# The first steps of a triangular inverse on compact 32x32 blocks instead of 128x128 matrices

## The chip, the cores and the metric

The kernel runs on one core of one Trainium2 chip. The metric is the device time of one execution in microseconds (us). A TensorE product is written as weights (lhsT) and a moving operand (rhs) and lands in PSUM; VectorE (DVE), ScalarE (ACT) and GpSimd (POOL) work on SBUF and PSUM, and the transfers from HBM are issued by SyncE (SP).

## The reference

One block and two further layers over 256 tokens of width 1024, in fp32. The block modulates a normed x, projects it, mixes it (a gMLP half and an RWKV7 half), and runs a mixture of 32 experts; the two layers are attention and a feed-forward part each. The change is inside the RWKV7 half, a recurrence over 256 steps for 8 heads of 64:

```python
def step(state, inp):
    r_t, w_t, k_t, v_t, a_t, b_t = inp
    sa = jnp.einsum('bhvk,bhk->bhv', state, a_t)
    state = (state * w_t[:, :, None, :] + sa[..., None] * b_t[:, :, None, :]
             + v_t[..., None] * k_t[:, :, None, :])
    return state, jnp.einsum('bhvk,bhk->bhv', state, r_t)
```

## The kernel before

The recurrence is computed in two chunks of 128 steps. Within a chunk the sa of each step depends on those of the steps before it through a strictly triangular 128x128 matrix N, so the kernel needs the inverse of I − N for each of 8 heads and 2 chunks, 16 matrices ("slots"). NT holds N transposed, for all slots side by side: a tile of 128 partitions and 16 times 128 columns. XT holds the inverse transposed as it grows, Y its transpose block by block.

The inverse is built by doubling. First come the 2x2 diagonal blocks, from N masked by offT plus the identity, made by POOL (L749, L750) one head at a time. Four levels follow, l from 1 to 4, which double the finished blocks to 4, 8, 16 and 32: a product N·Y (L782), a mask off[l] on it that keeps the new off-diagonal blocks and gives W (L798), a product X·W added to X (L800), and a transposition of the 32x32 blocks that gives Y for the next level (L791). Before, each of these works on whole 128x128 matrices in four groups of four slots (one PSUM bank, 512 columns), although of X and Y only the four 32x32 blocks on the diagonal hold anything yet. Behind the levels two further doublings go from 32 to 64 (the function blocks, L810, on 32x32 pieces of the array, with WC as the copy in between) and from 64 to 128 (L829 to L837). The finished XT is first used at L887.

The order of the instructions on each engine is made ahead of time by a scheduler that goes by priority and dependence; each engine then works through its list in order. Between the stages of the kernel stand fills: fill(n) draws n steps of a generator that computes modulation vectors, products of a vector with a weight matrix (L190), whose weights are loaded 1 MB at a time (wrows) into six slots. A step is 8 matmuls on four column strips of the array in turn. fill(FILL_A[2]), two steps, stands at the head of each level, fill(FILL_A[5]) behind them. A step's sum leaves PSUM through ACT (L230) or DVE (L232, ga), and after every fourth step DVE transposes the vector (L196, gt) and adds a bias (L197, modc). The same six slots, in program order, take the loads of the output projection and of the experts later.

The product L744 (AR, BP) makes N; L758 (AR, KP) makes the other matrix of the chunk, which DVE masks (L761, ma) and L765 and L766 multiply with V. These stand between the making of N and the first level.

## Time and profile before

| | |
|---|---|
| median of 3 runs | 1437.48 us (1435.19 to 1439.3) |
| profiled execution, its own time | 1440.6 us |
| its span in the trace | 1438.8 us |
| mean granted TensorE clock | 0.98 |
| TensorE busy | 94% of the span |
| VectorE busy | 53% |
| ScalarE busy | 40% |
| GpSimd busy | 5% |

The span runs from the first to the last instruction of the profiled execution; its own time has what lies around that. The shares are over the whole kernel, which has stages with very different limits, so what a change in one stage is worth must be read from the windows and timelines of that stage. An fp32 matmul leaves two records for its products (and two for its weight loads): counts of matmuls in the profile are twice those of the program. The granted clock is a share of 2.4 GHz, so that 0.50 is 1.2 GHz.

### The profile page before, as it was taken

What the parts mean: (1) busy time and instruction counts of PE and PEld (TensorE: products, weight loads), DVE (VectorE), ACT (ScalarE), POOL (GpSimd) and SP (SyncE); (2) the same over time, 40 slices, a digit from 0 to 9 for tenths busy, and PEclk for the clock granted to TensorE, in tenths of its full rate; (3) what the DMA queues carried; (4) which work ended last, traced back from release to release, by engine and by line L of the source; (5) the groups of instructions that cost most, each with busy time, mean ns of one, the idle gap of its engine ahead of it and who ended that gap; (6) DMA issues with size and microseconds to landing.
All of it is one profiled execution on the core that took longest, in us unless ns stands there. A gap on an engine that the chain in (4) does not pass through costs nothing.

```text
span 1438.8 us, 22940 instructions
## 1 busy us (share of the span) xinstructions
PE 1358.0 (94%) x9327; PEld 996.0 (69%) x9327; DVE 765.7 (53%) x1510; ACT 572.8 (40%) x1020; POOL 73.1 (5%) x77
## 2 busy tenths in 40 slices
PE   7989999999999988999889989999998999999997
PEld 5778887544443434444348867899996897799997
DVE  5639667511211111111165875888876575766565
ACT  3444013311110111111166765555456685655544
POOL 1002000000000000000020231000021001100000
PEclk9979999999999999999989999999999999999999
DMA  9817379699999999999956554978775434555540
GB/s 354 302 59 264 137 288 386 252 358 426 426 428 425 427 427 424 427 427 425 426 223 247 207 204 154 350 273 315 276 248 185 160 118 152 192 192 196 178 145 30
DMA packets 138690, 400.44 MB, mean 278 GB/s; under 512 B 6561, under 2 KB 84657, under 8 KB 114002
## 3 DMA queue, kind: packets, MB, share of 16 engines
q1 hardware_dynamic: 138578, 398.91, 72.1%
q8 instruction: 75, 1.23, 0.3%
q14 instruction: 37, 0.30, 0.1%
HBM read 397.82 MB, written 1.05 MB: 277 GB/s over the span
## 4 chain that ended last, share of the span: by engine, by line
PE 45%; DMA 9%; DVE 3%; ACT 2%; issue 1%; POOL 0%; POOLq 0%; DVEq 0%; SPq 0%; ACTq 0%
PE pmm L416 8%; PE pmm L417 8%; PE pmm L418 8%; PE pacc L416 5%; PE pacc L417 5%; PE pacc L418 5%; DMA wruns<-in_moe_w_down_dram 4%; DMA wruns<-in_moe_w_gate_dram 3%; DMA wruns<-in_moe_w_up_dram 3%; PE pmm L190 1%; PE pmm L1346 1%; PE pmm L1302 1%; DVE x_sb L1495 1%; PE pmm L366 1%; PE pmm L1705 1%
## 5 line engine op out<-in xcount | busy, mean ns | idle before, releaser
L416 PE MATMUL pmm<-hh,whi 128*128 128x256 f32 (+1 forms) x1040 | 296.0, 285 | 2.0 <-ACT whi L167 2.0
L418 PE MATMUL pmm<-hh,wlo 128*128 128x256 f32 (+1 forms) x1040 | 297.0, 286 | 0.0
L417 PE MATMUL pmm<-hl,whi 128*128 128x256 f32 (+1 forms) x1040 | 295.7, 284 | 0.0
L1302 PE MATMUL pmm<-wruns,xg 128*64 128x512 f32 x1024 | 232.6, 595 | 10.6 <-DMA wruns<-in_moe_w_gate_dram 9.0
L168 DVE TENSOR_TENSOR wlo<-wcols,whi 128x1024 fp32r<-128x1024 f32 (+1 forms) x130 | 168.4, 1300 | 97.4 <-ACT whi L167 96.9
L416 PEld LDWEIGHTS pmm<-hh,whi 128*128 128x128 f32 (+1 forms) x1040 | 197.5, 190 | 8.5 <-issue 3.6
L417 PEld LDWEIGHTS pmm<-hl,whi 128*128 128x128 f32 (+1 forms) x1040 | 196.6, 189 | 1.4
L418 PEld LDWEIGHTS pmm<-hh,wlo 128*128 128x128 f32 (+1 forms) x1040 | 197.1, 189 | 0.3
L167 ACT ACTIVATE whi<-wcols 128x1024 fp32r<-128x1024 f32 (+1 forms) x130 | 136.0, 1052 | 115.8 <-PE pmm L417 91.3
L1302 PEld LDWEIGHTS pmm<-wruns,xg 128*64 128x64 f32 x1024 | 75.3, 137 | 150.1 <-issue 127.6
L168 DVE TENSOR_TENSOR wlo<-wrows,whi 128x1024 fp32r<-128x1024 f32 x87 | 108.1, 1248 | 53.8 <-ACT whi L167 53.4
L167 ACT ACTIVATE whi<-wrows 128x1024 fp32r<-128x1024 f32 x87 | 91.6, 1061 | 89.6 <-PE pmm L417 46.4
L1346 PE MATMUL pmm<-wruns,em 128*64 128x512 f32 x512 | 118.8, 595 | 5.5 <-DMA wruns<-in_moe_w_down_dram 4.1
L1346 PEld LDWEIGHTS pmm<-wruns,em 128*64 128x64 f32 x512 | 38.3, 137 | 78.1 <-issue 61.3
L1355 ACT ACTIVATE o<-ay 128x512 fp32r<-128x512 f32 x32 | 20.2, 630 | 172.7 <-DVE ay L1354 172.7
L1354 DVE SCALAR_TENSOR_TENSOR ay<-pmm,wsl,ga 128x512 f32<-128x512 f32 x32 | 24.0, 751 | 101.7 <-PE pmm L1346 99.7
L1388 DVE TENSOR_TENSOR ay<-ay,pmm 128x512 f32<-128x512 f32 x16 | 11.0, 688 | 119.2 <-PE pmm L1302 105.8
L1333 DVE COPY wsl<-pmm 64x1 f32<-64x1 f32 x32 | 5.0, 156 | 126.6 <-PE pmm L1330 126.4
L417 PE MATMUL pacc<-wlo,ah 128*128 128x512 f32 x176 | 69.2, 393 | 0.0
L416 PE MATMUL pacc<-whi,ah 128*128 128x512 f32 x176 | 68.9, 391 | 0.0
L418 PE MATMUL pacc<-whi,al 128*128 128x512 f32 x176 | 68.6, 393 | 0.0
L1308 ACT ACTIVATE ay<-pmm 128x512 f32<-128x512 f32 x16 | 9.6, 598 | 109.3 <-PE pmm L1302 109.3
(530 smaller groups left out, 2190.2 us busy)
## 6 DMA issues: line engine op xcount, KB each, us to landing
wruns<-in_moe_w_gate_dram SPq DMA_DIRECT2D x64, 1024.0 KB, 19.5
wruns<-in_moe_w_up_dram SPq DMA_DIRECT2D x64, 1024.0 KB, 19.5
wruns<-in_moe_w_down_dram SPq DMA_DIRECT2D x64, 1024.0 KB, 19.6
wrows<-in_w_mod_dram SPq DMA_DIRECT2D x48, 1024.0 KB, 6.9
wcols<-in_w_ffn_gate_dram SPq DMA_DIRECT2D x22, 1024.0 KB, 5.1
wcols<-in_w_ffn_up_dram SPq DMA_DIRECT2D x22, 1024.0 KB, 7.2
wrows<-in_w_ffn_down_dram SPq DMA_DIRECT2D x22, 1024.0 KB, 4.9
wrows<-in_ada_w_dram SPq DMA_DIRECT2D x16, 1024.0 KB, 7.5
```

The source lines that it names most:

```text
L167: ACT.activation(hi, src, AF.Copy)
L168: (POOL if ahead else DVE).tensor_tensor(lo, src, hi.bitcast(F32), op=OP.subtract)
L190: PE.matmul(p[32 * g:32 * g + 32, 0:n].rearrange("p (a j) -> p a j", j=32), lhsT, groups(rhs)[:, g], start=first, stop=last, skip_group_ch ...
L366: PE.matmul(p, src[:, i, 128 * kt:128 * kt + 128], dg[i], start=True, stop=True)
L416: PE.matmul(p, a[0], b[0], start=first, stop=False, skip_group_check=True)
L417: PE.matmul(p, a[0], b[1], start=False, stop=False, skip_group_check=True)
L418: PE.matmul(p, a[1], b[0], start=False, stop=last, skip_group_check=True)
L1302: PE.matmul(p[64 * a:64 * a + 64, :], xg[:, kt, 128 * (j % 2) + 64 * a:128 * (j % 2) + 64 * a + 64], wt[a][:, k, :], start=kt == 0, stop=k ...
L1346: PE.matmul(pd[n][64 * a:64 * a + 64, :], hT[:, f, 64 * a:64 * a + 64], wt[a][:, b, 512 * n:512 * n + 512], start=f == 0, stop=f == 3, ski ...
L1354: DVE.scalar_tensor_tensor(yf, pd[n], wsl, ga2[:, ns], op0=OP.mult, op1=OP.mult)
L1355: ACT.activation(oh[:, ns], yf, AF.Copy)
L1495: DVE.scalar_tensor_tensor(xs, t[:, i, half_[n]], r[i], xs, op0=OP.mult, op1=OP.add)
```

## The change

The 2x2 blocks and the four levels are done on the diagonal 32x32 blocks alone. X3, Y3 and W3 hold them compactly, one tile of 128 partitions by 8 slots of 32 columns for each of two groups g of eight slots; block r of a matrix lies on partitions 32r to 32r+31. begin(g) copies the diagonal blocks out of NT with ACT, masks them, adds the identity and transposes, all on DVE; POOL's part goes. A level has two groups instead of four. products(g) runs 32 matmuls of 32x32x32 for a group, with the block r innermost: four in a row go to the four diagonal 32x32 places of the array and write four partition strips of one PSUM bank. DVE's operations on a level are 128x256 instead of 128x512, two of each kind instead of four. The masks off, offT are 128x32 (five instead of six), with an added identity idc. Behind the levels the products of the step to 64 read Y3 and X3 and are written slot by slot, so that two or three places of the array take turns; eight ACT copies bring the blocks of X3 into the full XT, which POOL has cleared, and four those of Y3 into a tile YW that holds Y and W of the last doubling.

On TensorE, before, a level and the fills around it stand like this (pacc<-wrows is a fill; each x16 of pmm is four groups of four slots); the first level has 6 of its 16 first products ahead of the fill:

```order
L190 MATMUL pacc<-wrows,par 32x256 x16
L782 MATMUL pmm<-Y,NT 128x128 x10
L782 MATMUL pmm<-XT,W 128x128 x16
L190 MATMUL pacc<-wrows,par 32x256 x16
L782 MATMUL pmm<-Y,NT 128x128 x16
```

In the same place after (Y_1569 and Y_1570, W_1571 and W_1572, X_1567 and X_1568 are Y3, W3 and X3 of the two groups; L806 is the product):

```order
L190 MATMUL pacc<-wrows,par 32x256 x16
L806 MATMUL pmm<-Y_1570,NT 32x32 x26
L806 MATMUL pmm<-X_1567,W_1571 32x32 x32
L806 MATMUL pmm<-X_1568,W_1572 32x32 x32
L190 MATMUL pacc<-wrows,par 32x256 x16
L806 MATMUL pmm<-Y_1569,NT 32x32 x32
L806 MATMUL pmm<-Y_1570,NT 32x32 x32
```

Each product has four times as many matmuls, and the first level has 38 of its 64 first products ahead of the fill.

On DVE, before, one level whose fill adds one vector (L232) looks like this, with W (L798), X (L800) and the transposes (L791):

```order
L232 TENSOR_TENSOR ga<-pacc,ga 128x256
L798 TENSOR_TENSOR W<-pmm,off 128x512 x4
L800 TENSOR_TENSOR XT<-pmm,XT 128x512
L791 STREAM_TRANSPOSE Y<-XT 128x512
L800 TENSOR_TENSOR XT<-pmm,XT 128x512 x2
L791 STREAM_TRANSPOSE Y<-XT 128x512
L800 TENSOR_TENSOR XT<-pmm,XT 128x512
L791 STREAM_TRANSPOSE Y<-XT 128x512 x2
```

And after (L814 is W, L817 is X, L752 the transpose):

```order
L232 TENSOR_TENSOR ga<-pacc,ga 128x256
L814 TENSOR_TENSOR W_1571<-pmm,off 128x256
L814 TENSOR_TENSOR W_1572<-pmm,off 128x256
L817 TENSOR_TENSOR X_1567<-pmm,X_1567 128x256
L752 STREAM_TRANSPOSE Y_1569<-X_1567 128x256
L817 TENSOR_TENSOR X_1568<-pmm,X_1568 128x256
L752 STREAM_TRANSPOSE Y_1570<-X_1568 128x256
```

There are 6 operations of half the width where there were 12; both W still stand behind the vector of the fill.

On ACT, before, from the last copies ahead of the levels (rh, yb) to the two copies behind them (WC, XT) and U, which follows L887:

```order
L769 ACTIVATE rh<-pacc 128x512
L770 ACTIVATE yb<-pacc 128x512
L230 ACTIVATE ga<-pacc 128x256 x2
L817 ACTIVATE WC<-pmm 32x512
L230 ACTIVATE ga<-pacc 128x256
L823 ACTIVATE XT<-pmm 32x16x32
L888 ACTIVATE U<-pmm 128x512
```

And after, where L850 copies blocks of X3 into XT, L838 blocks of Y3 into YW, L834 is WC and L847 the copy to XT from PSUM:

```order
L794 ACTIVATE rh<-pacc 128x512
L795 ACTIVATE yb<-pacc 128x512
L230 ACTIVATE ga<-pacc 128x256 x2
L850 ACTIVATE XT<-X_1567 32x2x4x32 x2
L838 ACTIVATE YW<-Y_1569 32x2x4x32 x2
L850 ACTIVATE XT<-X_1568 32x2x4x32
L838 ACTIVATE YW<-Y_1570 32x2x4x32 x2
L850 ACTIVATE XT<-X_1568 32x2x4x32
L850 ACTIVATE XT<-X_1567 32x2x4x32
L850 ACTIVATE XT<-X_1568 32x2x4x32
L850 ACTIVATE XT<-X_1567 32x2x4x32
L834 ACTIVATE WC<-pmm 32x512
```

Eleven copies of blocks stand ahead of WC now. SP's list is the same, and so are those of TensorE, DVE and ACT from the output projection on.

The diff:

```diff
--- before.py
+++ after.py
@@ -462,14 +462,18 @@
         oka = pool.tile([128, 4], F32, name="oka")
         DVE.tensor_scalar(oka, colr("k_a", 4), -1.0, 1.0, op0=OP.mult, op1=OP.add)
 
-        tI = pool.tile([128, 128], I32, name="tI")
-        sI = pool.tile([128, 128], I32, name="sI")
-        POOL.iota(tI, pattern=[[0, 128]], base=0, channel_multiplier=1)
-        POOL.iota(sI, pattern=[[1, 128]], base=0, channel_multiplier=0)
-        off = pool.tile([128, 6, 128], F32, name="off")
-        offT = pool.tile([128, 128], F32, name="offT")
-        mq = pool.tile([128, 128], F32, name="mq")
-        for l in range(6):
+
+        tI = pool.tile([128, 32], I32, name="tI")
+        sI = pool.tile([128, 32], I32, name="sI")
+        POOL.iota(tI, pattern=[[0, 32]], base=0, channel_multiplier=1)
+        POOL.iota(sI, pattern=[[1, 32]], base=0, channel_multiplier=0)
+        DVE.tensor_scalar(tI, tI, 31, None, op0=OP.bitwise_and)
+        idc = pool.tile([128, 32], F32, name="idc")
+        DVE.tensor_tensor(idc, tI, sI, op=OP.is_equal)
+        off = pool.tile([128, 5, 32], F32, name="off")
+        offT = pool.tile([128, 32], F32, name="offT")
+        mq = pool.tile([128, 32], F32, name="mq")
+        for l in range(5):
             DVE.tensor_tensor(off[:, l, :], tI, sI, op=OP.is_gt)
             if l == 0:
                 DVE.tensor_tensor(offT, sI, tI, op=OP.is_gt)
@@ -734,6 +738,27 @@
         pm = [pacc(), pacc()]
         py = [pacc(), pacc()]
         two = lambda m: m[:, None, :].to_broadcast([128, 2, 128])
+        POOL.memset(XT, 0.0)
+
+        X3, Y3, W3 = ([pool.tile([128, 8, 32], F32, name=f"{n}3{g}") for g in range(2)] for n in "XYW")
+        R4 = [slice(32 * r, 32 * r + 32) for r in range(4)]
+        heads = lambda a, r, g: a[R4[r]].rearrange("p (c h) t -> p c h t", c=2)[:, :, 4 * g:4 * g + 4, 32 * r:32 * r + 32]
+        h4 = lambda a: a.rearrange("p (c h) t -> p c h t", c=2)
+        bc = lambda m: m[:, None, :].to_broadcast([128, 8, 32])
+        flat = lambda a: a.rearrange("p c t -> p (c t)")
+
+        def turn_blocks(g):
+
+            DVE.transpose(out=flat(Y3[g]), in_=flat(X3[g]))
+
+        def begin(g):
+
+            for r in range(4):
+                ACT.activation(h4(W3[g][R4[r]]), heads(NT, r, g), AF.Copy)
+            DVE.tensor_tensor(X3[g], W3[g], bc(offT), op=OP.mult)
+            DVE.tensor_tensor(X3[g], X3[g], bc(idc), op=OP.add)
+            turn_blocks(g)
+
         for q in range(4):
             fill(FILL_A[0])
             for e in range(2):
@@ -746,8 +771,8 @@
                 p4 = p.rearrange("p (c x t) -> p c x t", c=2, x=2)
                 DVE.tensor_tensor(NT[:, h::8, :], p4[:, :, 0, :], two(gt), op=OP.mult)
                 DVE.tensor_tensor(RB[:, h::8, :], p4[:, :, 1, :], two(ge), op=OP.mult)
-                POOL.tensor_tensor(XT[:, h::8, :], NT[:, h::8, :], two(offT), op=OP.mult)
-                POOL.tensor_tensor(XT[:, h::8, :], XT[:, h::8, :], two(ident), op=OP.add)
+            if q % 2:
+                begin(q // 2)
         for q in range(4):
             fill(FILL_A[1])
             for e in range(2):
@@ -771,68 +796,68 @@
 
         gv.append(pacc)
 
-        Y, W = b8("Y"), b8("W")
-        G4 = [slice(4 * g, 4 * g + 4) for g in range(4)]
-        v4 = lambda a: a.rearrange("p (c t) -> p c t", t=128)
-        bc = lambda m: m[:, None, :].to_broadcast([128, 4, 128])
+        place = lambda g, s: 8 * (s // 4) + 4 * g + s % 4
 
         def products(g, lhsT, rhs):
-            p = pmm()
-            for sl in range(4):
-                PE.matmul(p[:, 128 * sl:128 * sl + 128], lhsT[:, 4 * g + sl, :],
-                          rhs if len(rhs.shape) == 2 else rhs[:, 4 * g + sl, :], start=sl == 0, stop=sl == 3,
-                          skip_group_check=True)
-            return v4(p)
-
-        flat = lambda a: a.rearrange("p c t -> p (c t)")
-
-        def turn_blocks(g):
-
-            DVE.transpose(out=flat(Y[:, G4[g]]), in_=flat(XT[:, G4[g]]))
-
-        for g in range(4):
-            turn_blocks(g)
+
+            p = pmm()
+            for s in range(8):
+                for r in range(4):
+                    PE.matmul(p[R4[r], 32 * s:32 * s + 32], lhsT(s, r), rhs[g][R4[r], s, :], start=s == 0, stop=s == 7,
+                              skip_group_check=True)
+            return p[:, 0:256].rearrange("p (c t) -> p c t", t=32)
+
         for l in range(1, 5):
             fill(FILL_A[2])
-            for g in range(4):
-                DVE.tensor_tensor(W[:, G4[g]], products(g, NT, Y), bc(off[:, l, :]), op=OP.mult)
-            for g in range(4):
-                DVE.tensor_tensor(XT[:, G4[g]], products(g, W, XT), XT[:, G4[g]], op=OP.add)
-            for g in range(4):
+            for g in range(2):
+                pn = products(g, lambda s, r: NT[R4[r], place(g, s), 32 * r:32 * r + 32], Y3)
+                DVE.tensor_tensor(W3[g], pn, bc(off[:, l, :]), op=OP.mult)
+            for g in range(2):
+                pn = products(g, lambda s, r: W3[g][R4[r], s, :], X3)
+                DVE.tensor_tensor(X3[g], pn, X3[g], op=OP.add)
                 turn_blocks(g)
 
         fill(FILL_A[5])
+        YW = b8("YW").rearrange("p a b -> p (a b)")[:, 0:1024].rearrange("p (s t) -> p s t", t=64)
+        Y, W = YW[0:64], YW[64:128]
+        POOL.memset(Y[0:32, :, 32:64], 0.0)
         v32 = lambda a: a.rearrange("p (c t) -> p c t", t=32)
         WC = pool.tile([128, 16, 32], F32, name="WC", tag="tmp2", bufs=3)
-
-        def blocks(p, o, lhsT, rhs):
-            for sl in range(16):
-                PE.matmul(p[o:o + 32, 32 * sl:32 * sl + 32], lhsT[:, sl, :], rhs[:, sl, :], start=sl == 0, stop=sl == 15,
-                          skip_group_check=True)
-
         sub = lambda a, r, c: a[r:r + 32, :, c:c + 32]
+        by_half = lambda a, g: a.rearrange("p (c h) t -> p c h t", c=2)[:, :, 4 * g:4 * g + 4, :]
         p = pmm()
-        for b in (0, 64):
-            blocks(p, b + 32, sub(NT, b, b + 32), sub(Y, b, b))
+        for s in range(16):
+            g, k = s // 8, place(s // 8, s % 8)
+            for b in (0, 64):
+                PE.matmul(p[b + 32:b + 64, 32 * k:32 * k + 32], NT[b:b + 32, k, b + 32:b + 64], Y3[g][b:b + 32, s % 8, :],
+                          start=s == 0, stop=s == 15, skip_group_check=True)
         ACT.activation(WC[32:64], v32(p[32:64]), AF.Copy)
         DVE.tensor_copy(WC[96:128], v32(p[96:128]))
+        for g in range(2):
+            for b in range(2):
+                ACT.activation(by_half(Y[R4[b], :, R4[b]], g), h4(Y3[g][R4[b]]), AF.Copy)
         p = pmm()
-        blocks(p, 0, WC[32:64], sub(XT, 32, 32))
-        blocks(p, 64, WC[96:128], sub(XT, 96, 96))
-        blocks(p, 32, sub(XT, 32, 32), WC[32:64])
-        ACT.activation(sub(XT, 0, 32), v32(p[0:32]), AF.Copy)
+        for s in range(16):
+            g, k = s // 8, place(s // 8, s % 8)
+            for o, lhsT, rhs in ((0, WC[32:64, k, :], X3[g][32:64, s % 8, :]), (64, WC[96:128, k, :], X3[g][96:128, s % 8, :]),
+                                 (32, X3[g][32:64, s % 8, :], WC[32:64, k, :])):
+                PE.matmul(p[o:o + 32, 32 * k:32 * k + 32], lhsT, rhs, start=s == 0, stop=s == 15, skip_group_check=True)
         DVE.tensor_copy(sub(Y, 32, 0), v32(p[32:64]))
         DVE.tensor_copy(sub(XT, 64, 96), v32(p[64:96]))
+        ACT.activation(sub(XT, 0, 32), v32(p[0:32]), AF.Copy)
+        for r in (2, 3, 0, 1):
+            for g in range(2):
+                ACT.activation(heads(XT, r, g), h4(X3[g][R4[r]]), AF.Copy)
         for g in range(2):
             p = pmm()
             for sl in range(8):
-                PE.matmul(p[64:128, 64 * sl:64 * sl + 64], NT[0:64, 8 * g + sl, 64:128], Y[0:64, 8 * g + sl, 0:64],
+                PE.matmul(p[64:128, 64 * sl:64 * sl + 64], NT[0:64, 8 * g + sl, 64:128], Y[:, 8 * g + sl, :],
                           start=sl == 0, stop=sl == 7, skip_group_check=True)
-            DVE.tensor_copy(W[64:128, 8 * g:8 * g + 8, 0:64], v3(p[64:128]))
+            DVE.tensor_copy(W[:, 8 * g:8 * g + 8, :], v3(p[64:128]))
         for g in range(2):
             p = pmm()
             for sl in range(8):
-                PE.matmul(p[0:64, 64 * sl:64 * sl + 64], W[64:128, 8 * g + sl, 0:64], XT[64:128, 8 * g + sl, 64:128],
+                PE.matmul(p[0:64, 64 * sl:64 * sl + 64], W[:, 8 * g + sl, :], XT[64:128, 8 * g + sl, 64:128],
                           start=sl == 0, stop=sl == 7, skip_group_check=True)
             DVE.tensor_copy(XT[0:64, 8 * g:8 * g + 8, 64:128], v3(p[0:64]))
 
```

## Rows read from the trace of the kernel before

**Rows 1.** Page: span, TensorE busy, mean busy share of the transfers in 40 slices.

```profile
span 1438.8 us, 22940 instructions
...
PE 1358.0 (94%) x9327; PEld 996.0 (69%) x9327; DVE 765.7 (53%) x1510; ACT 572.8 (40%) x1020; POOL 73.1 (5%) x77
...
DMA  9817379699999999999956554978775434555540
```

**Rows 2.** Windows (us, busy and count by engine, clock, DMA share, GB/s): levels, behind them, later MoE.

```profile
158.20:193.70 35.50, 35.50 (x373) 31.29 (x372) 30.52 (x55) 1.81 (x5) 0.00 (x0) 1.00 0.67 239
193.70:210.20 16.50, 16.05 (x332) 11.86 (x331) 9.94 (x20) 1.56 (x3) 0.00 (x0) 1.00 0.86 305
340.00:400.00 60.00, 60.00 (x302) 25.27 (x300) 13.31 (x24) 9.10 (x16) 0.00 (x0) 1.00 1.01 426
```

**Rows 3.** Timeline of PE (start, length, work, count, wait): end of masking, two levels.

```profile
149.73 0.43 PE L765 MATMUL pacc<-V,ma 128*128 128x64 f32 x2 [1.66 <-DVE ma L761]
...
155.75 1.05 PE L782 MATMUL pmm<-Y,NT 128*128 128x128 f32 x8
...
157.64 0.66 PE L782 MATMUL pmm<-Y,NT 128*128 128x128 f32 x4
158.23 1.93 PE L190 MATMUL pacc<-wrows,par 128*32 128x256 f32 x32
...
166.10 1.93 PE L190 MATMUL pacc<-wrows,par 128*32 128x256 f32 x32
167.96 3.84 PE L782 MATMUL pmm<-Y,NT 128*128 128x128 f32 x32
171.64 3.74 PE L782 MATMUL pmm<-XT,W 128*128 128x128 f32 x32
```

**Rows 4.** Timeline of DVE: transposes behind POOL, then operations inside the first two levels.

```profile
147.20 1.90 DVE L791 STREAM_TRANSPOSE Y<-XT 128x512 f32<-128x512 f32 x3 [3.23 <-POOL XT L750]
...
161.45 0.43 DVE L196 STREAM_TRANSPOSE gt<-ga 128x256 f32<-128x256 f32 x1
161.81 0.65 DVE L798 TENSOR_TENSOR W<-pmm,off 128x512 f32<-128x512 f32 x1
...
168.46 0.38 DVE L232 TENSOR_TENSOR ga<-pacc,ga 128x256 f32<-128x256 f32 x1
```

**Rows 5.** Timeline of PE: a full-array product, then the stretch behind the levels.

```profile
133.57 7.07 PE L744 MATMUL pmm<-AR,BP 128*128 128x256 f32 x32
...
193.71 1.93 PE L190 MATMUL pacc<-wrows,par 128*32 128x256 f32 x32
195.58 0.94 PE L810 MATMUL pmm<-Y,NT 32*32 32x32 f32 x24
196.45 0.62 PE L190 MATMUL pacc<-wrows,csil 128*32 128x256 f32 x2
...
199.27 2.01 PE L810 MATMUL pmm<-XT,WC 32*32 32x32 f32 x61
201.10 0.21 PE L810 MATMUL pmm<-WC,XT 32*32 32x32 f32 x1
...
201.21 1.08 PE L810 MATMUL pmm<-WC,XT 32*32 32x32 f32 x29
...
204.61 2.07 PE L829 MATMUL pmm<-Y,NT 64*64 64x64 f32 x32 [0.45 <-DVE Y L824]
...
210.19 2.00 PE L887 MATMUL pmm<-rh,XT 128*128 128x64 f32 x16
```

**Rows 6.** Timeline of ACT behind the levels.

```profile
198.38 0.59 ACT L817 ACTIVATE WC<-pmm 32x512 f32<-32x512 f32 x1 [12.35 <-PE pmm L810]
199.39 0.38 ACT L230 ACTIVATE ga<-pacc 128x256 f32<-128x256 f32 x1 [0.42 <-PE pacc L190]
```

**Rows 7.** Windows again, then timeline of PE: the stretch with a lower clock and what went ahead.

```profile
78.00:84.00 6.00, 6.00 (x18) 4.54 (x17) 0.00 (x0) 3.21 (x8) 0.00 (x0) 0.50 0.58 175
...
74.69 1.98 PE L603 MATMUL pmm<-w2a,twx 33*128 33x512 f32 x4
```

## Prediction made before the changed kernel was run

> **What bounds the kernel now.** I read the page first. TensorE (PE) is busy 94% of the span, and over long stretches so are the transfers: in the DMA row each digit is a slice of 36 us, and the fifth slice (144 to 180 us) has 3, the eighth (252 to 288) 6, those around them 7 to 9 [rows 1]. The windows of the stage come next. Between 158.2 and 193.7 us, the four levels of the inverse, PE is busy 35.50 of 35.50 us at a granted clock of 1.00, DVE 30.52, and the transfers move 239 GB/s; the stretch behind the levels is as full, at 305 GB/s, where the later MoE stretch moves 426 [rows 2]. So the stage waits for PE, and the transfers have room. The page's chain doesn't reach back to here, so I went by PE's own rows. A level is a fill of 32 records (an fp32 matmul leaves two), then 32 records of N·Y and 32 of X·W, without a gap: 167.96 − 166.10 = 1.86 us for the fill, 171.64 − 167.96 = 3.68 us for a product, or 115 ns a record; from the fill at 158.23 to that at 166.10 it is 7.87 us, because 12 records of this level were done ahead of it, from 155.75 on [rows 3]. From there to the fifth fill at 193.71, 35.48 us pass, and 16.48 more to the first matmul that uses the finished inverse, 210.19 [rows 3, 5]. PE waits once ahead of the levels, 1.66 us for a masked product of DVE, which stood behind three transposes that had waited 3.23 us for POOL's building of XT [rows 3, 4].
>
> **Which time.** The profiled execution took 1440.6 us (span 1438.8), 3.1 more than the median 1437.48. I sum differences and take them off both.
>
> **The price of a small matmul.** This decides everything. At one place of the array, 32x32x32 records come every 30 ns: 61 in 199.27 to 201.10 [rows 5]. The full array needs 115 ns for 128 columns [rows 3], so 30 ns is a quarter of it, as 32 columns are. Nothing is gained by smallness alone: a group of 16 records becomes 64 at a quarter of the time. The gain must come from the four diagonal places working at once. Two rows speak of that. The fill's matmuls use four column strips in turn: 1.93/32 = 60 ns a record of 256 columns, against 7.07/32 = 221 ns on the full array, 3.7 to 1 [rows 3, 5]. And between 201.10 and 201.21 a scheduler's accident alternates two places of different rows and columns in one PSUM bank: seven starts, six steps, 0.11/6 = 18 ns each [rows 5]. Four places would give 30/4 = 7.5 ns if they go on like the strips; the other end is 18 ns if two is all that overlap, and 30 ns if none do. I take 8 ns, near the 3.7 to 1 of the fill, since that is four-fold alternation as well, and keep the others as rivals.
>
> **Ahead of the levels.** POOL's 16 operations and the four 128x512 transposes go; ACT copies and three DVE operations of 128x256 for each of two halves come. ACT has nothing else to do then. PE's wait of 1.66 us goes, and 12 records of 115 ns (1.38 us) become the 76 that stand ahead of the first fill, 0.6 us. That is 2.4 us; the second half's operations stand between DVE's masked products, behind ACT copies, and may hold PE up to half a microsecond (estimate: one 0.4 us copy more than there is room for). I take −2.2, between −1 and −2.6. The smaller masks sit at the start, where the transfers are 9 tenths busy in the first slice [rows 1]: nothing.
>
> **A level.** Count from the start of a fill. PE: fill to 1.86, two products N·Y of 64 records, 0.51 each, to 2.9. DVE's addition of the fill starts 2.36 after the fill (168.46 − 166.10) and takes 0.38; an operation of 128x256 occupies DVE 0.36 (161.45 to 161.81) [rows 4]. So the first W runs 2.72 to 3.1, the second to 3.45. X·W can start when its W is there: 3.2 to 3.7, and 3.7 to 4.2. The X sums and transposes of a level, 4 × 0.36 = 1.4 us, lie under the next fill of 1.86. A level is thus 4.2 us, with 0.3 us in which PE waits for W; where two additions, a transpose and a small one stand ahead of W (every second fill closes a set of modulation columns) about 4.7, except in the first level, whose first W is ready ahead. Sum 4.1 + 4.2 + 4.7 + 4.2 = 17.2 against 35.48: −18.2. DVE's own work in a level, 6 × 0.36 and up to 1.3, stays under 4.2, so it isn't the bound by itself. If a record costs 12 ns, each level is about 1 us longer.
>
> **Behind the levels.** The 64 and 96 small records now alternate two and three places: 18 ns or less instead of 30. The new part is a wait. ACT makes eleven of its twelve 32x256 copies of X3 and Y3 ahead of the copy WC, though they stand behind it in the code; WC waited for PE alone before, 4.67 us after the fifth fill [rows 5, 6]. I estimate a copy at 0.38, since a 128x256 one took that and the 32x512 one 0.59 [rows 6]. The first X3 is there when the fifth fill starts, so ACT is free for WC 4.3 us later (0.1 + 11 × 0.38) and done at 4.9, while PE has finished its 32 products and five matmuls of the next fill at about 3.6. PE waits there some 1.3 us. From 4.9 on: eight fill matmuls at 0.116, 0.9; 94 records of 18 ns, 1.7; eight fill matmuls, 0.9; the two 64-wide products, 2.07 each as before [rows 5], 4.2; twelve fill matmuls, 1.4. That ends at 14.0 against 16.48. Four fill matmuls fewer stand here and are paid later, 0.2. So −2.3, between −1 and −3; with no copies in WC's way it would be −3.6.
>
> **Afterwards.** From the output projection on every engine's order is the same. The transfers of the MoE weights are asked for when slots come free, and the 6 of the eighth slice says that they wait for that [rows 1]; they start earlier by what the stage saves, and the transfer-bound stretch behind them moves as a whole. Sum: 2.2 + 18.2 + 2.3 = 22.7. From 1440.6 that is 1417.9, from the median **1415**.
>
> **Two rules against it.** The rows above show 18 ns between starts in one bank. The Trainium skill (TensorE: Matmul & The Clock Gate, "Wait — 56ns, not 53.3ns?") says that starts never come closer than about 25 ns however few the columns; by it a level is 1.86 + 256 × 0.025 = 8.3 us and the time about 1431. The row disagrees with it. The Trainium skill (TensorEngine Tiling (Array Packing), "Gotcha 1: PSUM Pressure") also says that different row tiles can't use one PSUM bank at the same time, which the new products do throughout; by it nothing would overlap, as in the fourth rival. The same row disagrees for two places; for four no row speaks.
>
> **Rivals.**
> First, *two at once, or PE's instructions don't come fast enough.* 18 ns a record: product 1.15, level 1.86 + 4.6 = 6.46, W hidden; four are 25.8, less the 76 records ahead (1.4): 24.5, −11.0. Ahead of the levels −1.6, behind −1.5. 1423. For it: 18 ns is the fastest that any row shows, and only for six steps. Against: the strips' 3.7 to 1.
>
> Second, *transfers.* Over both stretches of rows 2, 239 × 35.5 + 305 × 16.5 = 13.5 MB, 31.7 us at 426 GB/s; they would now last 17.3 + 14.1 = 31.4. Six loads of 1 MB lie ready when the stage begins, so I see no wait inside it, but two late loads would cost 2 × 2.46: about 1420.
>
> Third, *the clock.* From 78 to 84 us the clock was 0.50 (1.2 instead of 2.4 GHz) after PE had run matmuls of 33 rows; it stayed busy without a gap [rows 7]. The levels become such work. One such spell of 6 us costs 3; half clock throughout makes a level 2 × (1.86 + 2.05) = 7.8, four 30 with those ahead taken off: 1428. Against: the single-place records of 195 to 201 us stood between fills, and that stretch kept 1.00 [rows 2, 5].
>
> Fourth, *no overlap.* 30 ns: level 9.54, four 38.2 − 2.3 = 35.9, +0.4; −0.8 ahead, −0.5 behind: 1437, the change does nothing.
>
> Fifth, *slower: matmuls of four row strips hold one another at the shared bank.* It decides from 31 ns a record. The 24 records right behind the fifth fill took 196.45 − 195.58 = 0.87 us, 36 ns each, the slowest such row [rows 5]: level 11.1, four 44.3 − 2.7 = 41.6, +6.1, and 160 records behind, +1.0: 1444. A hold for a record's whole length (0.21, the row at 201.10) would be far worse, but there six others start before it has ended.
>
> **Numbers.** The forecast 60% (1411 to 1419 with 7.5 to 12 ns), two at once 16%, transfers 8%, clock 6%, no overlap 6%, slower 4%. A measurement of this kernel tells some 0.3%, 4.3 us, from no change. Faster 0.91 (the first four, and 1 in 6 of no overlap, for a pitch somewhat under 30), same 0.05, slower 0.04. The range 1410 to 1428 takes in the forecast, two at once, the transfers and half of the clock's case.
>
> **What would show it.** From the first level's fill to the fifth fill, about 17 us; 32x32 records at 8 ns, 0.5 us for 64; in each level a PE wait for W of 0.3 to 0.8; one wait of PE for WC of ACT near 1.3; no POOL wait of DVE; the clock at 1.00; transfers near 0.9 in the stage; the first use of the inverse 22 us earlier, and the same distance from there to the end. A pitch of 15 ns or more makes it wrong by 5 us and up; a clock under 1.00, or a gap of PE on a load, by what it lasts.

## The result, and the profile after the change

The changed kernel takes 1451.78 us, the median of four runs (1449.73 to 1456.32), beside 1436.34 us for the kernel before on the same chip: a ratio of 1.0112, 95% interval 1.0079 to 1.0145. It is slower by 11 to 21 us. The prediction, 1415 us with 0.91 on faster, was wrong in sign. The profiled execution took 1456.32 us, 15.7 more than that of before.

The page of the changed kernel, as in [rows 1], with the clock by slice and the queue that brings instructions:

```profile
span 1454.5 us, 24452 instructions
...
PE 1355.4 (93%) x10095; PEld 985.0 (68%) x10095; DVE 744.6 (51%) x1485; ACT 580.1 (40%) x1040; POOL 64.1 (4%) x63
...
PEclk9999868799999999999989999999999999999999
...
q8 instruction: 81, 1.33, 0.3%
```

PE is busy 2.6 us less over a span that is 15.7 us longer, so some work was exchanged for waiting (and part of what is left ran at a lower clock, as the windows below show). PE's row count grew by 768, each a matmul with its weight load. The instruction queue moved six more packets, 81 where the page of before has 75, and 0.10 MB more. That is about 16 KB a packet, and 256 instructions (768 × 2 / 6). In the forecast I had not looked at this line of the page.

The timeline of PE (start, length, work, count, wait), from the first masked product to the first use of the inverse, against [rows 3, 5]:

```profile
128.10 7.07 PE L769 MATMUL pmm<-AR,BP 128*128 128x256 f32 x32
...
150.65 1.93 PE L190 MATMUL pacc<-wrows,par 128*32 128x256 f32 x32
152.51 0.62 PE L806 MATMUL pmm<-Y,NT 32*32 32x32 f32 x50
152.95 0.19 PE L806 MATMUL pmm<-X,W 32*32 32x32 f32 x1
...
153.91 0.67 PE L806 MATMUL pmm<-X,W 32*32 32x32 f32 x54 [0.19 <-DVE W L814]
158.36 0.37 PE L806 MATMUL pmm<-X,W 32*32 32x32 f32 x10 [3.78 <-issue]
158.66 3.15 PE L190 MATMUL pacc<-wrows,par 128*32 128x256 f32 x32
161.74 1.35 PE L806 MATMUL pmm<-Y,NT 32*32 32x32 f32 x128
163.01 0.98 PE L806 MATMUL pmm<-X,W 32*32 32x32 f32 x84
167.93 0.83 PE L806 MATMUL pmm<-X,W 32*32 32x32 f32 x44 [3.94 <-issue]
...
178.02 1.15 PE L806 MATMUL pmm<-X,W 32*32 32x32 f32 x77 [3.87 <-issue]
...
187.44 1.16 PE L806 MATMUL pmm<-X,W 32*32 32x32 f32 x110 [3.59 <-issue]
188.53 4.04 PE L190 MATMUL pacc<-wrows,par 128*32 128x256 f32 x32
...
197.38 0.21 PE L844 MATMUL pmm<-WC,X 32*32 32x32 f32 x1 [1.16 <-issue]
...
209.84 3.68 PE L912 MATMUL pmm<-rh,XT 128*128 128x64 f32 x16
```

Two things are to be seen. The small matmuls are as fast as hoped: 50 starts in 0.44 us (152.51 to 152.95), 8.8 ns a record, and 128 in 1.27 us (161.74 to 163.01), 9.9 ns, right behind the first stop. But in every level PE stands still for 3.6 to 3.9 us, each time in the middle of a product whose inputs are there; the releaser is "issue", which means that PE waited for nothing that the profile shows. The stops don't stand at one place of a level. They come after 118, 84, 51 and 18 of the 128 records of X·W. Counted between the first two stops, 10 + 32 + 128 + 84 = 254 records have run, which with their weight loads are 508 instructions: about two packets of the instruction queue. The trace's DMA records hold these packets one by one, 16384 bytes each. The last ones ahead of the ends of the four stops (158.36, 167.93, 178.02 and 187.44 us) landed at 156.95, 166.64, 176.51 and 186.20, so PE resumes 1.2 to 1.5 us behind a landing. The records don't name the engine that a packet is for. In the profiles of the experiments below, too, every "issue" stop of PE that is shown ends 1.1 to 1.7 us behind the landing of such a packet.

Windows of PE alone (us, busy and count, granted clock, DMA share, GB/s), beside [rows 2]:

```profile
150.65:188.53 37.88, 22.22 (x1083) 0.86 0.63 224
158.66:161.74 3.08, 3.08 (x38) 0.59 0.12 39
198.80:226.10 27.30, 27.30 (x210) 0.50 0.50 184
270.30:284.00 13.70, 13.64 (x49) 0.50 0.97 394
```

And the first row of PE's waits by line (us in total, times, longest):

```profile
PE pmm L806 <- issue: 15.2, 4, 3.9
```

In the levels PE is busy 22.22 of 37.88 us, where it was busy all of 35.50 before. The fill behind the first stop ran at a clock of 0.59 and took 3.08 us instead of 1.86. And behind the stage, where PE had no gap, the clock was at its lower level (0.50, 1.2 GHz) for 27.30 us.

By place, in us, changed kernel minus before, from the rows above, [rows 3, 5] and the rows of xx further below:

| stretch | before | after | difference | forecast |
|---|---|---|---|---|
| start to the product AR,BP | 133.57 | 128.10 | −5.5 | 0 |
| to the first fill of a level | 24.66 | 22.55 | −2.1 | −2.2 |
| to the fifth fill (the levels) | 35.48 | 37.88 | +2.4 | −18.2 |
| to the product with xx, behind the output projection | 63.51 | 81.83 | +18.3 | −2.3 |
| from there to the end | 1181.6 | 1184.1 | +2.5 | 0 |

Most of the −5.5 is not the change's work: between 60 and 100 us the granted clock was 0.80 in the one profile and 0.96 in the other, by my estimate 40 × 0.16 = 6.4 us. In a second profile of each kernel the clock of this stretch was 0.83 in both, and AR,BP stood at 130.22 before and 128.89 after, 1.3 us apart.

### The profile page after: what moved, and what is told of

Read it like the earlier page. It is cut to its first block, busy times and chain, and to the rows that moved or that the text cites. A ratio compares the mean times of both kernels' runs of the same rounds, so it can differ in the third digit from the quotient of the medians.

```text
span 1454.5 us, 24452 instructions
## 1 busy us (share of the span) xinstructions
PE 1355.4 (93%) x10095; PEld 985.0 (68%) x10095; DVE 744.6 (51%) x1485; ACT 580.1 (40%) x1040; POOL 64.1 (4%) x63
## 4 chain that ended last, share of the span: by engine, by line
PE 47%; DMA 7%; DVE 3%; ACT 2%; issue 1%; POOL 0%; POOLq 0%; DVEq 0%; ACTq 0%; SPq 0%
PE pmm L416 8%; PE pmm L417 8%; PE pmm L418 8%; PE pacc L416 5%; PE pacc L417 5%; PE pacc L418 5%; DMA wruns<-in_moe_w_down_dram 3%; DMA wruns<-in_moe_w_gate_dram 3%; PE pmm L1327 2%; DMA wruns<-in_moe_w_up_dram 1%; PE pmm L1371 1%; PE pmm L190 1%; DVE x_sb L1520 1%; PE pmm L1296 1%; PE pmm L366 1%
```

## The experiments

My theory after the result: PE runs out of instructions in the levels (four stops, 15.2 us), and the lower clock follows from the stops. Rivals: the small matmuls themselves lower the clock, or something else takes the time behind the levels.

**one_place.** The four places are no longer visited in turn; all other instructions stay, so that a product runs slower and the instructions have more time to come.

```diff
-            for s in range(8):
-                for r in range(4):
+            for r in range(4):
+                for s in range(8):
```

> The changed kernel with its level products in another order: eight matmuls in a row at the same 32x32 place instead of four places in turn. Same instructions, same number. Theory (PE's instructions come in blocks of 256 and PE stops at every 512th when it uses them up faster than they arrive): at 30 ns a record, 256 instructions last 3.8 us, about as long as a stop, so the stops vanish or shrink under 1 us; a level is 9.6 us, the granted clock stays 1.00 in the levels and behind them, and the time is 1433 to 1443. Rival A (the clock falls because 32x32 matmuls are little work, not because PE stops): no stops, but half clock in the levels or behind them, 1450 or more. Rival B (the stops belong to the X.W product itself, which waits for something the profile doesn't show): a gap of 3.8 us stays in every level, 1455 or more.

Measured: 1454.77 us (1447.08 to 1460.84), ratio 1.0106 [1.0081, 1.0132]. Timeline of PE:

```profile
164.59 0.69 PE L806 MATMUL pmm<-X,W 32*32 32x32 f32 x10 [2.11 <-issue]
...
177.57 2.13 PE L806 MATMUL pmm<-X,W 32*32 32x32 f32 x44 [1.87 <-issue]
```

Window of PE over the levels:

```profile
155.97:204.80 48.83, 44.56 (x1085) 0.67 0.51 175
```

The stops stand at the same records (10, 44 and 77 are left behind them), but are 2.11, 1.87 and 0.29 us long, and the fourth is gone: the instruction stream sets the place, PE's pace the length. That speaks for the theory, though what I had expected of it, no stop over 1 us, a clock of 1.00 and 1433 to 1443 us, did not come; the time is that of rival A. Yet the clock was 0.67 over the levels although PE was busy 44.56 of 48.83 us. So it doesn't take the long stops to lower the clock, and the first rival is partly right; what lowers it in this run is not separated further.

**half.** The level's loops run for the first group alone; the levels of the second are left out.

```diff
-            for g in range(2):
+            for g in range(1):
```

> The changed kernel with the levels computed for the first group of eight slots only (products, masks, sums and transposes of the second group are left out). A level has 128 records of products and 32 of the fill instead of 288. Theory (a stop at every 512th instruction, that is every 255 or 256 matmul records): stops 255 records apart, so at most one in 1.6 levels, two in the four levels, each no longer than 3.9 us; 8 us or more come back from the stops. Rival B (the stop belongs to each level's X.W product): four stops, one in each level, in the same product. Levels' stretch 20 to 24 us by the theory, 28 or more by the rival.

Measured: 1440.56 us (1436.97 to 1444.88), ratio 1.003 [1.0017, 1.0044]. Timeline of PE:

```profile
160.18 0.66 PE L806 MATMUL pmm<-X,W 32*32 32x32 f32 x53 [1.80 <-issue]
...
166.04 0.43 PE L806 MATMUL pmm<-Y,NT 32*32 32x32 f32 x14 [3.12 <-issue]
...
171.93 0.64 PE L806 MATMUL pmm<-Y,NT 32*32 32x32 f32 x51 [0.92 <-issue]
...
177.97 1.06 PE L190 MATMUL pacc<-wrows,par 128*32 128x256 f32 x14 [3.19 <-issue]
```

Windows of PE over the levels and behind them:

```profile
155.00:179.60 24.60, 15.56 (x546) 0.93 0.97 382
179.60:203.50 23.90, 23.22 (x289) 0.50 0.41 133
```

With half the work of the levels gone, the kernel is still not faster than before (its time holds the wait for xx, found further below, as those of all kernels with compact blocks up to spread64 do). The stops now fall into X·W, N·Y and a fill alike, so no operand explains them. PE resumes at 160.18, 166.04, 171.93 and 177.97: 5.9, 5.9 and 6.0 us apart, one packet of 256 instructions each time (the trace has 254 or 255 of PE's in each step), while the transfers move 382 GB/s. I had expected at most two stops, one for every 512 instructions; there are four, one for every 256. And again a spell of 0.50, 23.90 us long, follows.

**pause.** The kernel before, with idle time in its levels and no more PE instructions: ten copies of W onto itself ahead of each level's X·W.

```diff
+                if g == 0:
+                    for _ in range(10):
+                        ACT.activation(W[:, G4[0]], W[:, G4[0]], AF.Copy)
```

> The kernel before, with ten ACT copies of the first group's W onto itself in each level, so that PE waits some 4 us for ACT ahead of X.W; no PE instruction is added. Theory (a stop of PE of this length makes the clock fall, and that costs more than the stop): the granted clock is 0.50 after each pause and in a stretch behind the levels, the mean clock falls from 0.98 to about 0.97, and the time rises by more than the 16 us of the pauses, to 1457 to 1475. Rival (the pauses cost only themselves, and the long half-clock stretch of the changed kernel has another cause): clock as before, 1450 to 1454.

Measured: 1465.57 us (1464.58 to 1466.76), ratio 1.0199 [1.0182, 1.0217]. The kernel's scheduler put fills into most of the pauses, so the idle times of PE came out uneven, 0.41, 0.88, 1.80 and 4.14 us. Timeline of PE:

```profile
204.16 6.53 PE L782 MATMUL pmm<-XT,W 128*128 128x128 f32 x32 [4.14 <-ACT W L801]
```

Windows of PE ahead of the end of that wait, around it and behind it:

```profile
179.00:203.00 24.00, 19.23 (x211) 1.00 0.94 374
203.00:209.80 6.80, 5.64 (x26) 0.50 1.02 429
213.20:250.80 37.60, 33.73 (x301) 0.50 0.19 62
```

Through the three shorter waits the clock stayed at 1.00; within the long one, which began at 200.0, it fell to 0.50 for 6.80 us, so a wait of that length costs the clock with full-size matmuls too. In the changed kernel the clock falls in the same way at 157.8, 168.0, 178.2 and 188.5 us, between 0.6 us ahead of the end of a stop and 1.1 behind it. The 37.60 us at 0.50 begin 9 us later in this run, among 32x32 products and shorter waits; which of these brought them it doesn't tell. With one_place, long stops are not the only way to a lower clock.

**burst.** 32 matmuls of the full array behind the levels, results unused: does heavy work right there keep the clock?

```diff
+        pb = pmm()
+        for i in range(32):
+            PE.matmul(pb[:, 0:256], NT[:, 0, :], flat(X3[1]), start=i == 0, stop=i == 31, skip_group_check=True)
```

> The changed kernel with 32 full-array matmuls of 256 columns (NT by X3, into a bank that nothing reads) between the last level and the fifth fill: 64 records, 6.9 us of dense work at full clock. Theory (the half clock behind the levels comes from the little work and the stops in them, and dense work ends it): the clock is 1.00 from the burst on, the 27 us stretch of half clock is gone, and the 5 us lost behind the levels and most of the 16 us lost later come back against the 7 us added: 1438 to 1449. Rival (the half clock behind the levels belongs to the work there and returns after the burst): 1455 or more, with a long stretch of 0.50 behind it.

Measured: 1469.94 us (1466.31 to 1473.46), ratio 1.0221 [1.0194, 1.0249]. I had mis-sized the burst; a record of 256 columns takes 229 ns, so it is 14.63 us long. Timeline of PE:

```profile
198.36 14.63 PE L822 MATMUL pmm<-X,NT 128*128 128x256 f32 x64
221.03 0.20 PE L847 MATMUL pmm<-WC,X 32*32 32x32 f32 x1 [2.63 <-issue]
```

Windows of PE over the burst and behind it:

```profile
199.50:220.00 20.50, 18.89 (x262) 1.00 0.26 91
220.00:240.50 20.50, 19.48 (x167) 0.50 0.52 178
```

The burst ran at full clock from 199.5 on, and the spell of 0.50 came behind it, with one more stop. Heavy work behind the levels doesn't buy the spell off.

**fills_behind.** The 32 fill records of each level but a few go behind the levels, and with them the loads that the fills set off.

```diff
-FILL_A = (0, 0, 2, 8, 0, 2)
+FILL_A = (0, 0, 0, 8, 0, 10)
```

> The changed kernel with the eight steps of fills taken out of the levels and put behind them (ten steps behind the levels instead of two). The six slots for weights are full, so hardly a transfer but those of instructions runs during the levels. Theory (instructions arrive at one block of 256 per 4 to 6 us whatever else is transferred): the levels' 2000 instructions of PE take 30 to 45 us even without a fill in them, with a stop about every second block, and the time is 1455 or more. Rival C (the blocks are late because they share the transfer engines with loads of 1 MB): the stops shrink under 1.5 us each, the levels take 16 to 22 us, and the time is 1445 or less.

Measured: 1454.35 us (1441.23 to 1458.62), ratio 1.0101 [1.0073, 1.0129]. Timeline of PE:

```profile
160.58 1.23 PE L806 MATMUL pmm<-Y,NT 32*32 32x32 f32 x109 [2.13 <-issue]
164.41 1.71 PE L806 MATMUL pmm<-X,W 32*32 32x32 f32 x109 [2.35 <-issue]
...
168.29 1.70 PE L806 MATMUL pmm<-Y,NT 32*32 32x32 f32 x110 [0.80 <-issue]
172.18 1.72 PE L806 MATMUL pmm<-X,W 32*32 32x32 f32 x112 [1.96 <-issue]
```

Window of PE over the levels:

```profile
152.67:181.68 29.01, 18.16 (x1040) 0.66 0.02 5
```

This is the cleanest reading of the supply. With the transfers quiet (5 GB/s) PE resumes every 3.83 to 3.89 us: 256 instructions in 3.87 us, 15 ns an instruction, 30 ns a matmul with its weight load. However fast the array takes small matmuls, over these packets they average no less than 30 ns. Beside the loads of half it was 5.9 us, or 46 ns. The packet itself is not what the loads stretch: it took 0.9 to 1.0 us there and 0.9 to 1.5 here; it starts later, and why is open. The levels still took 29 us with hardly a fill among them, a little less than the 30 to 45 that I had expected, and the stops came at every packet instead of every second one.

**after_again.** The changed kernel once more, beside the last two.

> The changed kernel once more, beside the kernel before on the same chip, to see how far a profile of it differs from the first: stops at the same instructions (255 matmul records apart, of 3 to 4 us), half clock behind the levels for 20 us or more, 1449 to 1457.

Measured: 1447.19 us (1446.36 to 1455.77), ratio 1.0091 [1.0064, 1.0119]. The stops stand at the same records (4.40, 3.72, 3.90 and 3.62 us), but behind the stage there is no long spell, against my expectation of 20 us or more: the window of PE there reads

```profile
196.20:244.00 47.80, 45.24 (x564) 1.00 0.94 355
```

From AR,BP to the product with xx this execution takes 132.2 us (128.89 to 261.09), the first 142.3, before 123.65. So the stops are a fixed part of the loss and the spell behind them a changing one of some 10 us; ten runs of the changed kernel lie between 1446.4 and 1456.3.

**wide64.** The same idea with half the instructions: diagonal blocks of 64x64, two places of the array, for all five levels (the step to 64 works on blocks of 32 inside them). The core of the edit:

```diff
-                for r in range(4):
-                    PE.matmul(p[R4[r], 32 * s:32 * s + 32], lhsT(s, r), rhs[g][R4[r], s, :], start=s == 0, stop=s == 7,
+                for r in range(2):
+                    PE.matmul(p[R2[r], 64 * s:64 * s + 64], lhsT(s, r), rhs[g][R2[r], s, :], start=s == 0, stop=s == 7,
```

> The changed kernel with 64x64 diagonal blocks held compactly instead of 32x32: two blocks to a matrix, 32 matmuls of 64x64x64 for a product at two places in turn, half as many instructions in a level (320 of PE) and DVE operations of 128x512, two of each kind. Theory (instructions): 320 in about 6 us is 53 a us, which the kernel before has in places without a stop, so no stop of over 1 us, clock 1.00 in the stage, a level of 6.0 to 6.3 us, 10 to 12 us less than before in the levels, 2 ahead of them, 2 to 4 behind: 1416 to 1427. Rival (the stops come with the turn between places of the array, whatever the number of instructions): stops as in the changed kernel, 1440 or more.

Measured: 1434.17 us (1427.75 to 1441.87), ratio 0.9985 [0.9969, 1.0]. Timeline of PE:

```profile
166.46 1.50 PE L807 MATMUL pmm<-XY,WB 64*64 64x64 f32 x44 [0.25 <-issue]
...
172.49 0.62 PE L807 MATMUL pmm<-XY,NT 64*64 64x64 f32 x13 [1.01 <-issue]
...
178.99 1.61 PE L807 MATMUL pmm<-XY,NT 64*64 64x64 f32 x46 [1.37 <-issue]
...
182.46 1.27 PE L190 MATMUL pacc<-wrows,par 128*32 128x256 f32 x17
```

Window of PE from the first fill of the levels to the first use of the inverse:

```profile
156.85:198.00 41.15, 36.02 (x912) 1.00 0.89 318
```

The matmuls do more work per instruction; the stops in the levels shrink to 0.25 to 1.37 us, with about 255 instructions from one to the next, and the clock stays at 1.00. The levels take 25.61 us (156.85 to 182.46) against 35.48. Supply it is, then. But the time is above the 1416 to 1427 that I had expected: the ten microseconds didn't reach the end, and something takes most of them back behind the stage.

**spread32 and spread64.** The instructions of the levels thinned with other work, the same in sum: the four groups of products AR,KP and V that stood ahead of the levels are put one into each level, with 32x32 and with 64x64 blocks.

```diff
-        for q in range(4):
+        def keys(q):
...
+            keys(l - 1)
```

> The changed kernel in another order: the products of AR with KP and of V with the masked matrix, which stood ahead of the levels, are done a quarter in each level, between N.Y and X.W. Same instructions, same operands. Theory (blocks of 256 instructions arrive every 3.9 us with free transfers and about every 6 us beside loads): a level has 624 PE instructions and 1.9 + 2.5 + 3.5 = 7.9 us of work, so the blocks still set its length, 9.5 to 14.6 us, but the stops are mostly filled with work that stood elsewhere: from the start of the product AR, BP to the fifth fill 47 to 58 us against 60 in the changed kernel, less half clock, 1432 to 1447. Rival (the stops belong to the order N.Y, X.W or to the 32x32 places): four stops of 3.8 us as before, no gain.

> The kernel with 64x64 blocks in the same order as the one before this: a quarter of the AR, KP and V products in each level. A level has 368 PE instructions and 1.9 + 4.1 + 3.5 = 9.5 us of work, 39 instructions a us. Theory: no stop of over 0.5 us in the levels, clock 1.00, from the start of the product AR, BP to the fifth fill 45 to 47 us against 48.5 without the spreading and 60 in the kernel before; 1424 to 1434. Rival (the stops come with the alternation of places, not with the rate): stops of 1.0 to 1.6 us as without the spreading, same time as it.

Measured: spread32 1438.27 us (1431.64 to 1444.36), ratio 1.0024 [1.0011, 1.0037]; spread64 1436.36 us (1431.81 to 1439.17), ratio 0.9994 [0.998, 1.0008]. Spreading the same four-place matmuls out takes 9 to 13.5 us off the changed kernel. In its profiled execution, the fastest of the twelve at 1431.64 us, the stops are down to 0.34 to 2.33 us and the clock is at 1.00 from 186.5 to 250 us. In spread64 no stop for instructions is left in the levels, and its clock is 1.00 from 150.9 to 250. From AR,BP to xx it needs 117.5 us (131.51 to 249.00), 6 less than before, and is yet no faster in all. So the loss behind has another cause.

**before_again and wide64_again.** Both once more, to tell what repeats.

> The kernel before once more, for a second profile: how long its stretches are when the clock's low spells fall elsewhere. By all theories the stretch from the product AR, BP to the first use of the inverse is 76 to 77 us, PE without a stop in the levels; what lies ahead of that product may be up to 6 us shorter than in the first profile, if its three low spells between 57 and 102 us were chance, and the span then 1433 to 1437.

> The kernel with 64x64 blocks once more, for a second profile. If the instruction blocks set its levels, the same stops of 1.0 to 1.6 us at the same instructions, and 66 to 67 us from the product AR, BP to the first use of the inverse. If its gain is lost later by chance low spells of the clock, the stretch from 230 to 270 us has another length than the first time; if it is lost to a wait that comes every time, the same one.

Measured: 1437.55 us and 1430.84 us, one execution each. In both profiles of wide64 PE waits for ACT's xx of the feature half, 2.06 and 2.07 us; in the kernel before it is 0.34. These are PE's rows with xx of before, of the changed kernel (with ACT's row ahead of it) and of wide64:

```profile
257.22 1.98 PE L1035 MATMUL pmm<-wfr,xx 128*128 128x36 f32 x16 [0.34 <-ACT xx L1052]
```

```profile
269.71 1.08 ACT L1077 ACTIVATE xx<-pmm 128x512 f32<-128x512 f32 x2 [1.61 <-DVE pacc L1010]
...
270.36 3.62 PE L1060 MATMUL pmm<-wfr,xx 128*128 128x36 f32 x16 [2.07 <-ACT xx L1077]
```

```profile
251.74 3.29 PE L1060 MATMUL pmm<-wfr,xx 128*128 128x36 f32 x16 [2.06 <-ACT xx L1077]
```

ACT waits for a product of DVE (L1010, with ga) whose result it doesn't read. In the instructions of before this copy waits for PE alone; in all kernels with small masks it waits for DVE as well. The masks stand early in a pool, so shrinking them moves each later tile; if xx now lies in memory that DVE's product still reads, this wait is what must come of it, and putting the tiles back must take it away.

**wide64_pad and spread64_pad.** An unused tile puts the later tiles back where they lay; nothing else changes.

```diff
+        pool.tile([128, 640], F32, name="pad")
```

> The kernel with 64x64 blocks and one unused tile of 2560 bytes beside its masks, which are that much smaller than before, so that every tile behind them lies where it lay before. Theory: the 2.1 us that PE waits near 250 us for ACT's copy xx, in every changed kernel and not before, is ACT waiting for DVE to release the memory in which xx now lies; with the padding ACT waits for PE alone, PE's wait falls to 0.3 us as before, and the time falls by 2 to 4 us against the same kernel without padding, to 1429 to 1433. Rival (the later loss is only the low spell of the clock that follows, which falls where it will): same wait or same time, 1434.

> The same unused tile in the kernel with 64x64 blocks and the AR, KP and V products spread over the levels. Theory: PE's wait for xx falls from 2.1 to 0.3 us and the time by 2 to 4 us, to 1432 to 1435. Rival: no change, 1436.

Measured: wide64_pad 1429.32 us (1423.69 to 1434.17), ratio 0.9954 [0.9935, 0.9973]; spread64_pad 1431.79 us (1427.62 to 1433.91), ratio 0.9968 [0.9957, 0.998]. Both are faster than the kernel before, by 0.5% and 0.3%, and each by 4.6 to 4.9 us faster than without the tile (by the ratios 0.3%, 3.7 to 4.5 us). The clock behind the wait has its part in that: 0.52 over 14.26 us in wide64, 0.76 over 14.11 in wide64_pad. PE's wait is back at 0.35 in wide64_pad, and so the place of the tiles is shown as its cause:

```profile
244.89 1.98 PE L1061 MATMUL pmm<-wfr,xx 128*128 128x36 f32 x16 [0.35 <-ACT xx L1078]
```

**compact32_pad.** The same in the changed kernel: its levels with 32x32 blocks stay as they are, the compact tiles are views of one large tile, XT is taken later, and a tile of 960 columns sets the place.

```diff
+        pool.tile([128, 960], F32, name="pad")
...
-        NT, RB, XT = b8("NT"), b8("RB"), b8("XT")
+        NT, RB, XY = b8("NT"), b8("RB"), b8("XY")
```

> The changed kernel's levels as they are (four 32x32 pieces a step, the same number of instructions), with the tiles of the stage laid so that ACT's xx of the feature half lies again in memory that only PE used before it, as in the kernel before. Theory (stops of PE for instructions and the half clock cost most of the 15 us, the place of xx the rest): the wait of 2.07 us for ACT xx falls to about 0.3, the stops of 3.6 to 4.4 us in the levels stay where they were, and the time falls by 2 to 5 us, to 1444 to 1450, ratio to before 1.005 to 1.009, still slower than before. Rival (the place of xx cost nothing of its own beside the clock): 1447 to 1455, ratio 1.009 to 1.012, as the changed kernel. Second rival (the place of xx was all that was lost): 1434 to 1440.

Measured: 1446.05 us (1441.79 to 1456.52), ratio 1.0076 [1.0048, 1.0103]. Timeline of PE:

```profile
263.19 1.98 PE L1064 MATMUL pmm<-wfr,xx 128*128 128x36 f32 x16 [0.34 <-ACT xx L1081]
```

Windows of PE over the levels and behind the wait for xx:

```profile
153.80:193.58 39.78, 26.35 (x1161) 0.79 0.58 198
263.19:278.00 14.81, 13.18 (x61) 0.77 0.87 348
```

The wait is 0.34 again, and the stretch behind it runs at 0.77, as the kernel before does in the same place, where the changed kernel had 0.50 for 13.70 us. The stops in the levels remain (3.64, 2.89, 5.06 and 1.27 us). So the place of xx takes the wait away here too; what that is worth in time is not shown, since the medians differ by 1 to 6 us and the intervals overlap. What is left, 0.0076 × 1436.85 = 10.9 us, I put down to the levels: the stops, and the clock in them and behind them.

## Why the prediction was wrong

**The step that failed is "A level"**, −18.2 us. Its mechanism, four places at once, was right: 8.8 to 9.9 ns a record where I took 8, and neither of the two rules that I had weighed against it shows in these rows. Its bound was missing. I summed PE's pace, DVE's operations and the fill, and took for granted that instructions arrive as fast as PE can run them. 288 records of a level are 576 instructions, two and a quarter packets; at 3.87 us a packet undisturbed that is 8.7 us, at 5.9 beside loads 13.3, against 8.87 us for a level before (35.48 / 4). The levels measured 9.47 us each. Even at the faster of these paces 0.2 us a level was all there was to gain. Against the forecast the levels miss by 20.6 us (+2.4 for −18.2); the stretch behind them misses by as much (+18.3 for −2.3), and that is the clock's and xx's part, below.

My first rival had named it ("or PE's instructions don't come fast enough"), but I priced both halves of it by the 18 ns of [rows 5], which are six steps inside one packet. A row shorter than a packet says nothing of a supply by packets. The 30 ns of the single place, in the same group, stand over 61 records, 122 instructions, and so say nothing of it either. The Trainium skill (Runtime: NRT & Kernel Launch, "Instruction fetch mechanics") says that a queue of the engine's own brings 16 KiB blocks of 256 instructions, and that crossing a block's edge is mostly hidden. The size agrees with the packets here; hidden it was not, with 15.2 us of stops in one stage.

**The clock** was my third rival, at 1418 to 1428, for small matmuls that lower it in the levels. It came in the levels (0.86 over them) and, larger, in a place that I had not thought of: at 0.50 from 198.80 to 226.10, behind the levels, some 13.7 us of loss at the two levels of the clock. In after_again this spell is missing and the levels themselves are slower (41.15 us, 151.43 to 192.58). The pause run shows that a long wait of PE can lower the clock without small matmuls; why one execution has the spell behind the levels and another not, no run here settles.

**Ahead of the levels** was right: −2.1 against −2.2.

**Behind the levels**: the wait of 1.3 us for WC behind eleven copies doesn't show. ACT was done with the eleven copies at 193.17, 4.6 us after the fifth fill began, and then itself waited 0.58 us for PE, whose fill had taken 3.97 us instead of 1.87, most of it at 0.50. In its place stand a stop of 1.16 us and the lower clock.

**Afterwards**, forecast at 0 because every engine's order was unchanged. The order was; the waits were not. Smaller masks moved xx, PE's wait went from 0.34 to 2.07 us, and the clock behind it stayed at 0.50 for 13.70 us, where the kernel before has 6.80 (262.0 to 268.8). That took 4.6 to 4.9 us from the two 64x64 kernels. This error is a second one of its own: with the levels right I would still have been off by it.

**The sum.** From AR,BP to xx the changed kernel lost 18.6 us: about 13.7 by the spell of low clock behind the levels, 1.7 by xx, 1.2 by the last stop, 2.4 in the levels, less 2.1 ahead of them; that leaves 1.7. Two more spells at 0.50 lie in this stretch, 188.5 to 191.9 and 253.3 to 256.8, where the kernel before was at 1.00; by half their length they cost some 1.7 us each, so these terms more than cover the loss.

## What to carry to other kernels

Before cutting matmuls into smaller ones, count PE's instructions in the stretch and set them against the pace at which they can arrive, here 256 in 3.9 to 6 us, over a run longer than that number; pieces twice as large gave the gain that the smallest pieces lost (with the later tiles back in place), and thinning the smallest with heavier work took most of the loss away. When a change alters tile sizes, compare the waits of later instructions too, not only their order: the same order can wait for another engine. The fastest version, wide64_pad at 0.9954 of before, has the larger pieces and the old places; spread64_pad, at 0.9968, has the thinning as well.

## What the runs showed of the hardware

PE's instructions came in packets of 16384 bytes (six more packets for 1536 more instructions), and where PE ran out of them it resumed 1.1 to 1.7 us behind the landing of one: every 3.87 us with quiet transfers, every 5.9 to 6.0 us beside 382 GB/s. In the changed kernel the stops came after every second packet, in half and fills_behind after each; why is open. A PE that is busy without a gap can still be at 0.50: 27.30 us in one execution of the changed kernel, none there in another, with the same stops at the same records. Four row strips that write one PSUM bank in turn started 8.8 ns apart.
